# A two-layer encoder trunk on one core: two accumulator banks for the recurrence alone, and its attention and gate work put under it by priority

## The chip, the core and the metric

The kernel runs on one NeuronCore of a Trainium2 chip. The metric is the time of one execution in device microseconds: a median of 1884.04 us in three runs of the kernel before (1882.89 to 1890.43). The engines have short names here: PE is the matrix engine and PEld its weight load, DVE the vector engine, ACT the scalar engine, POOL the GpSimd engine, SP the engine that issues most of the loads.

## The reference

Two layers over 512 tokens of width 1024, all in float32. Cut to what matters:

```python
xn = rms_norm(x, ln1[l]);  z = xn @ w_in[l]
a_q, a_i, a_ff, a_fb, a_g, b_u, b_v, c_q, c_k, c_v, gz = split(z)
# branch A: gated linear recurrence, forward and backward, 4 heads of 128
y_a = rms_norm(hgrn2_bidirectional(a_q, a_i, a_ff, a_fb, lower[l]), a_norm[l]) * silu(a_g)
# branch B: u * (W_s LN(v) + b) with a 128x128 mixing matrix per group
y_b = spatial_gating(gelu(b_u), gelu(b_v), w_s[l], b_s[l])
# branch C: windowed attention, 8 query heads, 2 key heads, blocks of 128, a sink per head
y_c = window_attention(rope(c_q), rope(c_k), c_v, sink[l])
g = sigmoid(gz)                                   # three gates of width 1024
x = x + (g[0]*(y_a @ w_br[l,0]) + g[1]*(y_b @ w_br[l,1]) + g[2]*(y_c @ w_br[l,2])) @ w_out[l]
x = x + square(relu(rms_norm(x, ln2[l]) @ w_up[l])) @ w_down[l]
```

A last rms_norm ends the program.

## The kernel before

**Wide products.** Each float32 operand is split into a rounded high part and the rest, so that a product is three matmuls: high by high, high by rest, rest by high (lines 172 to 174 and 200 to 202). A projection (`proj`, `proj_w`) takes one 128 x 1024 weight chunk and gives one 128 x 512 tile in an accumulator bank tagged "m", by 24 matmuls of 512 columns (12 for a `yB` tile). Its weight chunk is loaded by SP into one of two `wr` buffers, cast by ACT (line 166) and subtracted by DVE (line 168).

**Banks.** The eight accumulator banks are dealt out by tag: "m" for projections (3), "a" for branch A (1), "c" for scores of branch C and parts of the larger products (2), "s" for transposes, norms and the outputs of C (2). A tile takes a bank of its tag and holds it until its last reader is done.

**One layer** runs through four parts: the large token-wise products of the input projection (names tA to gC, pool "G"), the three branches (pool "br"), the merge (pool "Y2": names `y`, `mT`, `wo`), and the MLP (names `up`, `dA` to `dC`). The branch part is where the change lies. It has these pieces:

- **A head of branch A** (`a_ffb`, then `a_head`): two gate projections `f`, one `q`; then eight products `at` of 128 x 128 blocks, one after the other. Between two of them stand an exponential on ACT for `qt` and one for `kt` (lines 513, 516), a multiplication on DVE (514), a masked copy of the product (504) and two in-place updates of `ex` on DVE (541). Then come a transpose `kT`, states `stp`, the output `av`, a norm over ACT, DVE and POOL, and a transpose `oT`. There is one `ex` buffer and one `at` buffer, so the heads follow each other.
- **Branch B**: `gelu2` and a norm of `bv`, mixing products `mx`; its merge, `gz` and `yB` for eight column blocks d, gives `mg`, which POOL stores to memory (`mgd`).
- **Branch C**: four runs j of four blocks n. `c_scores` makes two score tiles `sc` and their softmax (DVE line 831, ACT line 835, DVE 838 to 842); `c_out`, one step later, transposes (`pT`), copies (ACT line 858), multiplies (`po`, line 862) and copies out (864).
- **Gates of A**: four projections `ag` with a tanh.

**What sets the order.** The program is recorded through a scheduler that fills each engine's list by its own time table: of the instructions it holds ready, the one with the lowest priority number is next. The number is the place in the source text; `hp()` lifts a block to the front. The lists are fixed at build time; on the chip every engine takes its list strictly in order, each instruction waiting for its own semaphores. In the source before, the order is head 0, branch B, head 1, branch C whole, head 2, head 3, the merge of B, the gates of A.

## Time and profile before

| what | value |
|---|---|
| median of three runs | 1884.04 us |
| the profiled execution, its own time | 1884.62 us |
| its span, first to last instruction | 1882.8 us |
| PE busy in the span | 1763.8 us, 94% |
| DVE busy | 1316.7 us, 70% |
| ACT busy | 1010.8 us, 54% |
| branch part of layer 0, first `f` to first `y` | 176.4 to 505.5 us |
| branch part of layer 1 | 1077.7 to 1433.8 us |

The span and the profiled execution's own time differ by 1.8 us, which lies around the first and last instruction. Busy time of PE is modelled from overlapping matmuls, so it says where PE waits rather than how much of its rate is used. Views used below: the busy time of each engine in chosen stretches ("windows"), with the granted clock of PE (1.00 is full speed); the list of instructions in order of time ("timeline"), where `x8` counts matmuls, a float32 one as two passes, and the brackets give the idle time ahead of an instruction and what ended it; and groups of like instructions.

### The profile page before, as it was taken

Reading aid. Unit: us, or ns where it says so; the run is one execution under the profiler, and the core shown is the slowest. Engines: PE = TensorE matmul, PEld = TensorE weight load, DVE = VectorE, ACT = ScalarE, POOL = GpSimd, SP = SyncE. Lnnn points to the kernel's source line nnn. Section 1 sums busy time; section 2 is a strip of 40 time slices with the busy share of each in tenths; the row PEclk is TensorE's granted clock in tenths of the full one; section 3 lists DMA queues with packets and bytes.
Section 4 is the critical chain, followed back from the end, with each engine's and each line's share of the span. In section 5 each row is a group of like instructions: output and inputs, shape, how many; then the busy total and the mean of one; then the engine's idle time right before and its main releaser. Section 6 shows DMA issues by size and latency. Waiting matters only on the chain.

```text
span 1882.8 us, 21899 instructions
## 1 busy us (share of the span) xinstructions
PE 1763.8 (94%) x8032; PEld 1435.4 (76%) x8032; DVE 1316.7 (70%) x2006; ACT 1010.8 (54%) x1683; POOL 139.7 (7%) x183
## 2 busy tenths in 40 slices
PE   6999997999699999999989999979978999999997
PEld 4778876887587778888868888758866878888785
DVE  8886885577464767676887679856673656676857
ACT  4555664566323645454565576755772245545453
POOL 3010110000210000000010101101002100000000
PEclk8999997999799999999989999979997999999999
DMA  6242221212253342333334222203214442333221
GB/s 230 90 134 82 86 68 45 90 62 73 85 194 128 108 129 75 123 100 100 128 107 134 81 88 70 76 23 106 84 35 149 153 168 80 122 103 99 96 72 45
DMA packets 54698, 189.34 MB, mean 101 GB/s; under 512 B 7232, under 2 KB 7744, under 8 KB 54592
## 3 DMA queue, kind: packets, MB, share of 16 engines
q1 hardware_dynamic: 43776, 153.35, 24.5%
q0 software_dynamic: 10240, 33.56, 5.1%
q8 instruction: 63, 1.03, 0.2%
q10 hardware_dynamic: 576, 1.05, 0.1%
q14 instruction: 43, 0.35, 0.1%
HBM read 171.15 MB, written 16.78 MB: 100 GB/s over the span
## 4 chain that ended last, share of the span: by engine, by line
PE 61%; issue 25%; DVE 7%; ACT 5%; DMA 1%; POOL 1%; SPq 0%; POOLq 0%; DVEq 0%; ACTq 0%
PE up L174 3%; PE up L172 3%; PE up L173 3%; PE at L499 2%; PE y L200 2%; PE y L201 2%; PE y L202 2%; PE dA L380 2%; PE wo L200 2%; PE dA L381 2%; PE gz L172 2%; PE wo L202 2%; PE wo L201 2%; PE dA L382 2%; PE gz L173 2%
## 5 line engine op out<-in xcount | busy, mean ns | idle before, releaser
L168 DVE TENSOR_TENSOR wl<-wr,wh 128x1024 fp32r<-128x1024 f32 x172 | 210.5, 1224 | 198.7 <-ACT wh L166 198.3
L166 ACT CAST wh<-wr 128x1024 fp32r<-128x1024 f32 x172 | 180.3, 1049 | 289.4 <-PE up L173 101.4
L166 ACT CAST wh<-wq 128x1024 fp32r<-128x1024 f32 x196 | 205.6, 1049 | 228.5 <-PE dA L381 53.7
L168 DVE TENSOR_TENSOR wl<-wq,wh 128x1024 fp32r<-128x1024 f32 x196 | 239.0, 1221 | 119.3 <-ACT wh L166 117.7
L172 PE MATMUL up<-xh,wh 128*128 128x512 f32 x512 | 199.5, 391 | 3.7 <-ACT wh L166 3.7
L173 PE MATMUL up<-xl,wh 128*128 128x512 f32 x512 | 199.9, 390 | 0.0
L174 PE MATMUL up<-xh,wl 128*128 128x512 f32 x512 | 198.8, 390 | 1.1 <-DVE wl L168 1.1
L172 PEld LDWEIGHTS up<-xh,wh 128*128 128x128 f32 x512 | 96.1, 188 | 26.7 <-ACT wh L166 7.1
L174 PEld LDWEIGHTS up<-xh,wl 128*128 128x128 f32 x512 | 96.2, 188 | 21.7 <-DVE wl L168 1.9
L173 PEld LDWEIGHTS up<-xl,wh 128*128 128x128 f32 x512 | 96.2, 188 | 19.9 <-DVE xl L212 0.4
L380 PE MATMUL dA<-wh,sh 128*128 128x512 f32 x256 | 101.9, 398 | 0.2
L381 PE MATMUL dA<-wh,sh 128*128 128x512 f32 x256 | 100.8, 394 | 0.0
L499 PE MATMUL at<-qt,kt 128*128 128x128 f32 x448 | 71.3, 308 | 25.8 <-DVE at L504 8.9
L499 PEld LDWEIGHTS at<-qt,kt 128*128 128x128 f32 x448 | 65.7, 218 | 32.9 <-ACT kt L516 27.9
L382 PE MATMUL dA<-wl,sh 128*128 128x512 f32 x256 | 90.4, 394 | 0.0
L541 DVE TENSOR_TENSOR ex<-ex 128x512 f32<-128x512 f32 x112 | 76.8, 703 | 7.2 <-ACT kt L516 6.5
L229 POOL TENSOR_TENSOR rs<-ms,mhalf_t 128x4 f32<-128x4 f32 x13 | 16.6, 1273 | 638.7 <-DVE ms L227 616.0
L380 PEld LDWEIGHTS dA<-wh,sh 128*128 128x128 f32 x256 | 48.1, 188 | 14.6 <-ACT wh L166 3.7
L513 ACT ACTIVATE qt<-ex 128x512 f32<-128x512 f32 x56 | 37.8, 675 | 38.9 <-DVE ex L541 34.6
L831 DVE CUSTOM_DVE_ANT_0 sc<-sc,cmask_t,snk_t 128x256 f32<-128x256 f32 (+1 forms) x64 | 34.5, 545 | 33.9 <-PE pT L857 33.7
L382 PEld LDWEIGHTS dA<-wl,sh 128*128 128x128 f32 x256 | 48.1, 188 | 10.9
L381 PEld LDWEIGHTS dA<-wh,sh 128*128 128x128 f32 x256 | 48.3, 189 | 10.6
(383 smaller groups left out, 4471.2 us busy)
## 6 DMA issues: line engine op xcount, KB each, us to landing
wr<-in_ws_dram SPq DMA_DIRECT2D x172, 512.0 KB, 3.3
wq<-in_ws_dram SPq DMA_DIRECT2D x112, 512.0 KB, 4.3
thd<-zt POOLq DMA_DIRECT2D x32, 256.0 KB, 2.7
th<-thd POOLq DMA_DIRECT2D x32, 256.0 KB, 4.4
mgd<-mg POOLq DMA_DIRECT2D x16, 256.0 KB, 2.4
mB<-mgd POOLq DMA_DIRECT2D x16, 256.0 KB, 3.5
x<-in_xT_dram SPq DMA_DIRECT2D x8, 256.0 KB, 7.3
xr<-in_xt_dram POOLq DMA_DIRECT2D x8, 256.0 KB, 5.2
```

Source lines behind the costliest of these rows:

```text
L166: nc.scalar.copy(hi, raw)
L168: nc.vector.tensor_tensor(lo, raw, hi.bitcast(F32), ALU.subtract)
L172: nc.tensor.matmul(pt, whi, xhi, start=first, stop=False)
L173: nc.tensor.matmul(pt, whi, xlo, start=False, stop=False)
L174: nc.tensor.matmul(pt, wlo, xhi, start=False, stop=last)
L200: nc.tensor.matmul(pts[t], xh, hi[:, c], start=k == 0, stop=False)
L201: nc.tensor.matmul(pts[t], xl, hi[:, c], start=False, stop=False)
L380: nc.tensor.matmul(pts[p], xh[:, t], hi[:, c], start=start and k == 0, stop=False, skip_group_check=True)
L381: nc.tensor.matmul(pts[p], xl[:, t], hi[:, c], start=False, stop=False, skip_group_check=True)
L382: nc.tensor.matmul(pts[p], xh[:, t], lo[:, c], start=False, stop=k == 3, skip_group_check=True)
L499: nc.tensor.matmul(pt[:, c], kk(st), qq[:, c], start=True, stop=True)
L541: nc.vector.tensor_tensor(o_ap, o_ap, ap_of(ex, i_, [[istep, 2]] + z), ALU.add)
```

## The change

The change rewrites the order of the branch part and deals the banks anew.

- Banks: "m" goes from 3 to 2, "a" from 1 to 2. The large products take two "a" banks where they took one "m" and one "a".
- `a_head` gets a second `at` buffer.
- A class `later(n)` raises the priority number of what stands in it, so that it is placed behind text that follows it. Runs of branch C stand in `later(15000)`, the eight parts of B's merge (`merge_b`) and the gates of A (`gate_a`) in `later(30000)`.
- In the source the order is now: head 0, branch B and its split, head 1, C's keys and values, merge part 0, run 0, head 2, parts 1 and 2, run 1, part 3, head 3, part 4, run 2, parts 5 to 7, run 3, the last `c_out`, the gates of A.
- The gates' tiles move from tag "tv" to "l2". In the merge branch A is taken first and C second, where it was C and then A; the splits swap their pools (A's into Y2's "yi", C's into Y1's "yh").

The number of instructions is the same on every engine (7526 on PE, 1998 on DVE, 1561 on ACT with the table loads, 188 on POOL, 306 on SP), and so is each kind.

```diff
--- before.py
+++ after.py
@@ -82,8 +82,8 @@
 
     HOME = {t: p for p, ts in {"G": ("xs", "zt"), "Y1": ("yh",), "br": ("q", "a", "g", "ch"), "Y2": ("yi", "th", "mg"), "mlp": ("h",)}.items() for t in ts}
     part = {}
-    BANKS = {"m": 3, "a": 1, "c": 2, "s": 2}
-    GROUPS = (("m", "m", "c", "c"), ("m", "a", "s", "s"))
+    BANKS = {"m": 2, "a": 2, "c": 2, "s": 2}
+    GROUPS = (("m", "m", "c", "c"), ("a", "a", "s", "s"))
     WR, WB, NZ, NCT, NSM, NQ = 2, 2, 3, 4, 4, 10
 
     def nm(s):
@@ -114,6 +114,19 @@
         return ps.tile([P, S], F32, tag="p_" + tag, bufs=BANKS[tag], name=nm(name))
 
     hp = tc.high_priority
+
+    class later:
+
+
+        def __init__(self, n):
+            self.n = n
+
+        def __enter__(self):
+            tc.cur_priority += self.n
+
+        def __exit__(self, *e):
+            tc.cur_priority -= self.n
+
     cnt = [0]
 
 
@@ -397,7 +410,7 @@
                 V.tensor_tensor(b11[i], t1[i], b22[i], ALU.add)
         product(6, b11, pa, False)
         read("P16", pa)
-        pc = [PT("m", name + "C"), PT("a", name + "C")]
+        pc = [PT("a", name + "C") for _ in range(2)]
         product(7, t3, pc, True)
         read("P7", pc)
         product(5, t1, pa, False)
@@ -490,7 +503,7 @@
         return ex
 
     def a_head(l, h, ex, q, vt):
-        at = part["br"].tile([P, 4, P], F32, tag="at", bufs=1, name=nm("at"))
+        at = part["br"].tile([P, 4, P], F32, tag="at", bufs=2, name=nm("at"))
 
         def attn(kk, qq):
             pt = PT("a", "at")
@@ -768,9 +781,41 @@
             nc.vector.scalar_tensor_tensor(bu[g], y, 0.5, bu[g], ALU.mult, ALU.mult)
             yb.append(bu[g])
 
+        def y_split(ys, tag):
+            res = []
+            for y in ys:
+                hi, lo = T(tag, "yh", F32R), T(tag, "yl", F32R)
+                split(y, hi, lo)
+                res.append((hi, lo))
+            return res
+
+
+        ys = y_split(yb, "yh")
+        wbr = [None]
+
+        def merge_b(d):
+            z = evac(proj(xs, "gz", l, "gz", d), "z", "gz")
+            with hp():
+                nc.scalar.activation(z, z, AF.Tanh, scale=0.5)
+            if d % 2 == 0:
+                wbr[0] = wload(l, "yb", d // 2)
+            yp = proj_w(ys, "yB", wbr[0], (d % 2) * 4)
+            m = T("g", "mg")
+            with hp():
+                nc.vector.scalar_tensor_tensor(m, z, 1.0, yp, ALU.add, ALU.mult)
+            nc.gpsimd.dma_start(mgd[:, d], m)
+
+        sg = []
+
+        def gate_a():
+            z = evac(proj(xs, "ag", l, "ag", len(sg)), "l2", "ag")
+            th = T("jk", "th")
+            nc.scalar.activation(th, z, AF.Tanh, scale=0.5)
+            nc.vector.scalar_tensor_tensor(z, th, 1.0, z, ALU.add, ALU.mult)
+            sg.append(z)
+
         g1 = a_ffb(1)
         q1 = evac(proj(xs, "q", l, "q", 1), "q", "q")
-
         oa.append(a_head(l, 1, g1, q1, vt))
 
 
@@ -863,52 +908,42 @@
             for h, r in enumerate((lo64, hi64)):
                 nc.scalar.copy(yc[j][r, n * P:(n + 1) * P], po[r, h * P:(h + 1) * P])
 
+        def fill(*ds):
+            with later(30000):
+                for d in ds:
+                    merge_b(d)
+
+        def c_run(j):
+            nonlocal prev
+            with later(15000):
+                qs = c_q(j)
+                for n in range(4):
+                    cur = c_scores(j, n, qs)
+                    if prev is not None:
+                        c_out(*prev)
+                    prev = cur
+
         prev = None
-        for j in range(4):
-            qs = c_q(j)
-            for n in range(4):
-                cur = c_scores(j, n, qs)
-                if prev is not None:
-                    c_out(*prev)
-                prev = cur
-        c_out(*prev)
-
+        fill(0)
+        c_run(0)
         g2 = a_ffb(2)
         q2 = evac(proj(xs, "q", l, "q", 2), "q", "q")
         oa.append(a_head(l, 2, g2, q2, vt))
-
+        fill(1, 2)
+        c_run(1)
+        fill(3)
         g3 = a_ffb(3)
         q3 = evac(proj(xs, "q", l, "q", 3), "q", "q")
         oa.append(a_head(l, 3, g3, q3, vt))
-
-        def y_split(ys, tag):
-            res = []
-            for y in ys:
-                hi, lo = T(tag, "yh", F32R), T(tag, "yl", F32R)
-                split(y, hi, lo)
-                res.append((hi, lo))
-            return res
-
-
-        ys = y_split(yb, "yh")
-        for d in range(KT):
-            z = evac(proj(xs, "gz", l, "gz", d), "z", "gz")
-            with hp():
-                nc.scalar.activation(z, z, AF.Tanh, scale=0.5)
-            if d % 2 == 0:
-                wbr = wload(l, "yb", d // 2)
-            yp = proj_w(ys, "yB", wbr, (d % 2) * 4)
-            m = T("g", "mg")
-            with hp():
-                nc.vector.scalar_tensor_tensor(m, z, 1.0, yp, ALU.add, ALU.mult)
-            nc.gpsimd.dma_start(mgd[:, d], m)
-        sg = []
-        for h in range(4):
-            z = evac(proj(xs, "ag", l, "ag", h), "tv", "ag")
-            th = T("jk", "th")
-            nc.scalar.activation(th, z, AF.Tanh, scale=0.5)
-            nc.vector.scalar_tensor_tensor(z, th, 1.0, z, ALU.add, ALU.mult)
-            sg.append(z)
+        fill(4)
+        c_run(2)
+        fill(5, 6, 7)
+        c_run(3)
+        with later(15000):
+            c_out(*prev)
+        with later(30000):
+            for h in range(4):
+                gate_a()
         end("br")
         begin("Y2")
 
@@ -923,7 +958,7 @@
                 th = []
                 for t in range(4):
                     z = T("th", "th")
-                    nc.gpsimd.dma_start(z, thd[:, bi * 4 + t, fl * S:(fl + 1) * S])
+                    nc.gpsimd.dma_start(z, thd[:, (1 - bi) * 4 + t, fl * S:(fl + 1) * S])
                     th.append(z)
                 pts = proj_tok(ys, f"y{br}", (l, "y", br, fl), grp)
                 grp ^= 1
@@ -948,10 +983,10 @@
                             split(m, hi, lo)
                         ms[d] = (hi, lo)
 
-        gated(0, 2, y_split(yc, "yi"))
         for h in range(4):
             nc.vector.scalar_tensor_tensor(oa[h], oa[h], 0.5, sg[h], ALU.mult, ALU.mult)
-        gated(1, 0, y_split(oa, "yh"))
+        gated(0, 0, y_split(oa, "yi"))
+        gated(1, 2, y_split(yc, "yh"))
 
 
         xr = [[T("l", "xr"), T("l", "xr")] for _ in range(4)]
```

How the lists move, at three places of PE's list in the branch part of layer 0. The names: `at` is a level of a head of branch A, `kT`, `stp`, `av`, `oT` are its end; `q`, `gz`, `yB` are projections, `pT`, `sc`, `po` belong to branch C, `y` to the merge. "x4" are four matmuls that follow each other.

Head 1, before. The eight levels stand one behind the other, and the head's end behind them:

```order
L499 MATMUL at_1803<-qt_1798,kt_1801 128x128 x4
L499 MATMUL at_1813<-q_1795,dg_1811 128x128 x4
L499 MATMUL at_1826<-qt_1821,kt_1824 128x128 x4
L499 MATMUL at_1839<-qt_1834,kt_1837 128x128 x4
L499 MATMUL at_1852<-qt_1847,kt_1850 128x128 x4
L499 MATMUL at_1865<-qt_1860,kt_1863 128x128 x4
L499 MATMUL at_1878<-qt_1873,kt_1876 128x128 x4
L499 MATMUL at_1894<-qt_1889,kt_1892 128x128 x4
L556 MATMUL kT_1908<-id_t,kd_1906 128x128 x3
L561 MATMUL stp_1914<-vt_453,kT_1912 128x128
L561 MATMUL stp_1914<-vt_455,kT_1912 128x128
L561 MATMUL stp_1914<-vt_527,kT_1912 128x128
```

Head 1 in the change, around its third and fourth level:

```order
L187 MATMUL q_2430<-xh_156,wl_2428 128x512
L185 MATMUL q_2430<-xh_164,wh_2426 128x512
L512 MATMUL at_1842<-qt_1837,kt_1840 128x128 x4
L186 MATMUL q_2430<-xl_165,wh_2426 128x512
L187 MATMUL q_2430<-xh_164,wl_2428 128x512
L902 MATMUL pT_2300<-id_t,sc_2246 128x128 x3
L512 MATMUL at_1855<-qt_1850,kt_1853 128x128 x4
L185 MATMUL gz_2640<-xh_110,wh_2636 128x512
L186 MATMUL gz_2640<-xl_111,wh_2636 128x512
L185 MATMUL yB_2668<-yh_1690,wh_2182 128x512
L186 MATMUL yB_2668<-yl_1691,wh_2182 128x512
L187 MATMUL yB_2668<-yh_1690,wl_2184 128x512
```

Projections stand between the levels now. From the second to the last level there are 20, 2, 36, 24, 14 and 22 wide matmuls of `q`, `gz`, `yB` and `cq` between neighbours, and a few of C's; the gap of two wide ones is the one shown.

The end of the branch part, before. Behind the last pieces of head 3 stands its transpose, and then the merge at once:

```order
L584 MATMUL av_3382<-st_3356,qd_3360 128x128
L584 MATMUL av_3382<-st_3375,qd_3379 128x128
L584 MATMUL av_3382<-vt_529,at_3235 128x128
L584 MATMUL av_3382<-st_3356,qd_3360 128x128
L596 MATMUL oT_3405<-id_t,ao_3403 128x128 x4
L200 MATMUL y_884_4024<-wh_4030,yh_4000 128x512
L200 MATMUL y_885_4025<-wh_4030,yh_4000 128x512
```

In the change C follows the same transpose of head 3:

```order
L609 MATMUL oT_3262<-id_t,ao_3260 128x128 x4
L902 MATMUL pT_3504<-id_t,sc_3448 128x128 x3
L902 MATMUL pT_3509<-id_t,sc_3453 128x128 x3
L873 MATMUL sc_3726<-k_447_2127,q_796_3681 128x384
L874 MATMUL sc_3726<-kl_2129,q_796_3681 128x384
L907 MATMUL po_3514<-pT_3503,cvt_2144 128x256 x3
L902 MATMUL pT_3710<-id_t,sc_3487 128x128 x2
```

and the merge starts behind C's last block:

```order
L907 MATMUL po_3793<-pT_3782,cvt_2144 128x256 x3
L902 MATMUL pT_3822<-id_t,sc_3766 128x128 x3
L902 MATMUL pT_3827<-id_t,sc_3771 128x128 x3
L907 MATMUL po_3832<-pT_3821,cvt_2144 128x256 x3
L902 MATMUL pT_3839<-id_t,sc_3805 128x128 x2
L902 MATMUL pT_3843<-id_t,sc_3810 128x128 x2
L907 MATMUL po_3847<-pT_3838,cvt_2144 128x256 x2
L213 MATMUL y_884_4028<-wh_4034,yh_4004 128x512
L213 MATMUL y_885_4029<-wh_4034,yh_4004 128x512
```

Six outputs of C (`po`) with their transposes, and six of the score tiles, now stand between head 3's `oT` and the first `y`. In layer 1 it is six outputs too. Before, C's last three outputs stood between the first levels of head 3.

## The prediction

> **What bounds the kernel now.** I read the page first, then the windows of the branch part, then its timeline.
>
> ```profile
> span 1882.8 us, 21899 instructions
> PE   6999997999699999999989999979978999999997
> PEclk8999997999799999999989999979997999999999
> PE 61%; issue 25%; DVE 7%; ACT 5%; DMA 1%; POOL 1%; SPq 0%; POOLq 0%; DVEq 0%; ACTq 0%
> ```
>
> PE and its own issue make 86% of the chain, so time is won only where PE stands still or runs slowly. Outside the first slice the busy row dips in few places, and PEclk dips with it: both lie in the branch parts. Windows of those (layer 0: rows 1 to 4, layer 1: 5 to 8) and one of the MLP:
>
> ```profile
> core 0: us, PE busy (x) PEld busy (x) DVE busy (x) ACT busy (x) POOL busy (x), PEclk, DMA share, GB/s
> 177.00:300.00 123.00, 119.90 (x596) 100.85 (x595) 95.04 (x160) 73.68 (x121) 17.33 (x12) 0.99 0.27 90
> 300.40:329.45 29.05, 17.07 (x74) 14.38 (x72) 18.87 (x30) 13.51 (x27) 0.00 (x0) 0.57 0.06 18
> 329.45:463.00 133.55, 132.37 (x675) 111.79 (x676) 84.84 (x195) 83.78 (x199) 9.11 (x12) 0.98 0.22 75
> 463.00:505.50 42.50, 25.52 (x139) 20.65 (x137) 24.49 (x49) 22.01 (x60) 1.73 (x3) 0.81 0.04 13
> 1077.00:1227.90 150.90, 146.13 (x722) 122.02 (x721) 121.44 (x210) 100.94 (x157) 18.14 (x16) 0.99 0.25 81
> 1227.90:1256.20 28.30, 17.07 (x73) 14.15 (x72) 18.73 (x31) 14.85 (x28) 0.00 (x0) 0.65 0.10 34
> 1256.20:1394.40 138.20, 133.52 (x694) 112.45 (x692) 89.63 (x203) 95.88 (x216) 10.07 (x12) 0.98 0.22 73
> 1394.40:1435.70 41.30, 25.48 (x121) 20.76 (x122) 22.48 (x45) 20.03 (x56) 3.71 (x6) 0.74 0.07 23
> 860.00:880.00 20.00, 20.00 (x90) 16.55 (x89) 10.11 (x15) 9.26 (x15) 0.00 (x0) 1.00 0.37 127
> ```
>
> The last row gives the price of a wide matmul that nothing holds up: about 88 starts in 20 us, 0.227 us. Each layer has a **bare stretch** (rows 2 and 6: 29.05 and 28.30 us), where head 1 runs alone, and a **tail** (rows 4 and 8: 42.5 and 41.3 us), where head 3 runs with the last of C. The rest is full. Inside the bare stretch of layer 0, in order of time:
>
> ```profile
> 302.23 1.13 PE L499 MATMUL at<-q,dg 128*128 128x128 f32 x8 [0.77 <-ACT at L519]
> 304.81 2.05 PE L499 MATMUL at<-qt,kt 128*128 128x128 f32 x8 [1.45 <-DVE at L504]
> 308.35 2.05 PE L499 MATMUL at<-qt,kt 128*128 128x128 f32 x8 [1.49 <-DVE qt L514]
> 311.76 2.05 PE L499 MATMUL at<-qt,kt 128*128 128x128 f32 x8 [1.36 <-DVE at L504]
> 328.71 0.68 DVE L627 TENSOR_TENSOR q<-q,rb 128x512 f32<-128x512 f32 x1
> 329.45 0.79 PE L172 MATMUL gz<-xh,wh 128*128 128x512 f32 x1 [1.17 <-DVE q L627]
> 334.74 0.63 PE L172 MATMUL gz<-xh,wh 128*128 128x512 f32 x1
> 335.76 0.39 PE L172 MATMUL gz<-xh,wh 128*128 128x512 f32 x1
> ```
>
> Every level waits on DVE or ACT (the brackets), 3.4 us from one to the next (308.35 to 311.76), while its eight matmuls need about 0.9 us at full clock. Projections could have run there: the next, `gz`, waited for a bank (329.45, released by DVE line 627, the read of head 3's `q` at 328.71). All three "m" banks were held by projections whose readers waited for head 1 to free its buffers. After the stretch the wide matmuls run 0.43 us apart until about 335.2.
>
> **The change part by part.** No work is added or removed, so each stretch is worth its length less the work in it.
>
> *The bare stretches go.* In the lists, 2 to 36 wide matmuls now stand between head 1's levels. Layer 0: 29.05 us hold eight levels (7.2 us), three `kT` and six `stp` matmuls (0.85): 21.0 us are lost now. From 329.4 to 335.2, 14 matmuls take 5.8 us where 14 x 0.227 = 3.2 would do: 2.6 more. Layer 1: the 73 matmuls of row 6 are six levels (5.4 us), the same nine (0.85) and 16 wide ones (3.6): 18.4 of 28.3 us lost, and some ten slow matmuls behind it, 2.0. Together **-44.0 us**. The fill is no new work: it comes out of 329 to 463, which is full (PE busy 132.4 of 133.6 us), and shortens that by its own length. That a level with cover costs nothing, head 0 shows:
>
> ```profile
> 208.44 1.06 PE L499 MATMUL at<-q,dg 128*128 128x128 f32 x8
> 214.58 1.06 PE L499 MATMUL at<-qt,kt 128*128 128x128 f32 x8
> ```
>
> 6.1 us apart, no idle bracket.
>
> *The tails are dealt anew.* Head 3's end now, and C's steps where little else runs:
>
> ```profile
> 481.06 1.13 PE L499 MATMUL at<-qt,kt 128*128 128x128 f32 x8 [1.48 <-DVE qt L514]
> 484.57 1.16 PE L499 MATMUL at<-qt,kt 128*128 128x128 f32 x8 [2.38 <-ACT kt L516]
> 486.89 0.90 PE L556 MATMUL kT<-id_t,kd 128*128 128x128 f32 x3 [1.16 <-ACT at L533]
> 491.15 0.90 PE L556 MATMUL kT<-id_t,kd 128*128 128x128 f32 x3 [1.15 <-DVE st L568]
> 495.42 0.80 PE L584 MATMUL av<-vt,at 128*128 128x128 f32 x2 [1.15 <-DVE st L568]
> 503.16 1.09 PE L596 MATMUL oT<-id_t,ao 128*128 128x128 f32 x4 [3.40 <-DVE ao L592]
> 505.53 2.08 PE L200 MATMUL y<-wh,yh 128*128 128x512 f32 x4 [1.28 <-ACT yh L208]
> ```
>
> ```profile
> 1380.51 1.13 PE L862 MATMUL po<-pT,cvt 128*128 128x256 f32 x4
> 1383.39 1.03 PE L862 MATMUL po<-pT,cvt 128*128 128x256 f32 x4
> 1394.46 1.56 PE L862 MATMUL po<-pT,cvt 128*128 128x256 f32 x6 [1.23 <-ACT pT L858]
> 1398.50 1.56 PE L862 MATMUL po<-pT,cvt 128*128 128x256 f32 x6 [0.93 <-ACT pT L858]
> ```
>
> In the change the fill ends (last `ag`) with two levels of head 3 left in layer 0, one in layer 1. Layer 0: first level 0.4, next 3.5, to `kT` 2.3, to `av` 8.5, to `oT` 7.7, its own 1.1. The second "a" bank saves some 1.5, since the second `kT` no longer waits for the states' reads (491.15). That is 22.0 us. Then six outputs of C stand in PE's list before the merge. A two-block step takes 2.9 us (1380.51 to 1383.39), a three-block one 4.0, both at full clock; three of each make 20.7. At half clock their matmuls on the chain (about 1.0 and 1.6 us) double: 28.5. I take 24, between them, since PEclk is 0.81 and 0.74 in today's tails. With 1.3 for the first cast before `y` (505.53), 47.3 us. It holds 20.9 us of work: two levels 1.8, the head's end 4.2, 20 `po` products 8.6 (1.03 us covered a row of four passes), 40 transposes 3.3, ten score tiles 3.0. Lost: 26.4. Today's 42.5 us hold 16.9 (eight levels, three steps, the same end): 25.6. So +0.8. Layer 1: 43.7 less 20 is 23.7, against 41.3 less 13.8, 27.5: -3.8. Together **-3.0 us**; the bounds of a step's price make it -10 to +6.
>
> *New tight places.* A level needs 2.4 us between the end of the one before and its start (1.5 after the `dg` product, 304.81; `kT` 1.4 after the last level). Where the list has less cover, PE waits for the rest. Layer 0: 0.7 us of cover at the fourth level of head 1 (two wide matmuls, three transposes): 1.7; 0.4 at head 2's third: 1.1; `kT` of heads 0, 1 and 2 with 0, 0 and 1.1: 3.1. Layer 1 has five such places, 4.5. Together **+10.4 us**. Below lies 0, if cover elsewhere is longer than the chain needs; above 25, if the stretch loses as 177 to 300 does (its DVE is 77% busy) and these places besides.
>
> *One "m" bank fewer.* A read of a projection takes 0.68 us (328.71), and between a projection's end and the next but one's start stand 4 to 9 us of matmuls in most cases, 1.3 at least (`yB`). In the MLP the third `up` product must now wait for the first one's reader:
>
> ```profile
> 616.76 1.08 ACT L1018 ACTIVATE u<-up 128x512 f32<-128x512 f32 x2
> 616.91 0.50 PE L172 MATMUL up<-xh,wh 128*128 128x512 f32 x1 [0.43 <-ACT wh L166]
> ```
>
> That reader starts at 616.76, half of the pair; the third product starts at 616.91. So 0.5 us a layer, **+1.0**. If readers get late the cost is the rival below.
>
> *At nothing:* the swap of A and C in the merge (the same 192 matmuls a layer; both casts still precede the first `y`), the gates' tiles in "l2" (`bu` is split by then), the same number of table loads on ACT. SP brings weight chunks in another order, but one per 5.5 us of PE work as now. POOL's store of `mg` waits for DVE, and a head's `rs` and `dg` are queued behind it; head chains have cover except in the tail, where no store is left. If a store were late there, a head would slip by its 1 to 3 us.
>
> Sum: -44.0 - 3.0 + 10.4 + 1.0 = -35.6 us. Against the profiled execution's own 1884.62 us (median of the runs 1884.04, the same within 0.6) that is **1849 us**.
>
> **The clock, by the page.** In the bare stretch PE's idle gaps were 1.4 to 1.5 us (the brackets from 304.81 on), and still the granted clock fell to half:
>
> ```profile
> 305.00:310.00 5.00, 3.52 (x16) 3.25 (x16) 2.83 (x5) 1.64 (x3) 0.00 (x0) 0.50 0.09 35
> 310.00:320.00 10.00, 6.09 (x25) 5.29 (x25) 7.60 (x12) 3.88 (x7) 0.00 (x0) 0.50 0.00 0
> ```
>
> The Trainium skill ("TensorE: Matmul & The Clock Gate", section "Part 1: The HAM clock gate (the "warmup" mystery)") has the clock halved after at least one idle window of about 3.4 us. By that rule no gap of the new tail would halve it. The rows speak against so strict a reading.
>
> **Rivals.**
> - *The tail stays at full clock.* For it: today's tail holds 1.00 while C's steps are between the levels. Against: head 3's end runs at half there. Steps at 20.7 instead of 24 save 6.6 us in two layers, the head's end at full clock 4.2 a layer: **1834**. It is also what the page's rule would give.
> - *DVE becomes the bound under head 3*, whose levels now share it with C's steps, the weights and the gates.
>
> ```profile
> L541 DVE TENSOR_TENSOR ex<-ex 128x512 f32<-128x512 f32 x112 | 76.8, 703 | 7.2 <-ACT kt L516 6.5
> ```
>
> Between its first and seventh level DVE's list in the change holds 34 instructions of this size (23 of the head, 11 of the gates; 0.70 each), four subtractions twice as wide (1.4) and some 6 us of small ones of C: 35 us, where PE's list holds 27. For it: the neighbouring levels have 4 to 5 us of cover, no more. Against: 0.70 is latency, and neighbours overlap. If the head slips by the 8 us in each layer, **1865**.
> - *Two banks block (the slower side).* Two projections with late readers now suffice to hold PE, where it took three (329.45). Each such block costs what the bare stretch did, 21.0 + 2.6 us. One a layer gives back the gain and more: 1849 + 47 = **1896**; it decides from one block in each layer. Against: DVE's list has the reads of head 2's and 3's gate projections at the start of the head before, not behind its levels.
> - *The fill is in the list but late* (weights, casts): the bare stretch comes back elsewhere, **1884**.
>
> **How the numbers follow.** Forecast 0.62, full clock 0.10, DVE 0.15, blocks 0.07, no effect 0.06. A measurement of this kernel can tell about 0.5% (9.4 us) from no change. Faster 0.62 + 0.10 + 0.15 = 0.87, same 0.06, slower 0.07. The range takes in the tail's bounds (-7 to +9), the tight places' (-10 to +15) and the two faster rivals: 1828 to 1870.
>
> **What would show it.** Right: no stretch of head 1 with PE under 70% busy, PEclk near 1.00 from the first `f` to the last `ag`; one tail a layer of 44 to 47 us, in which six `po` rows follow head 3's `oT` 3 to 5 us apart; idle before `at` and `kT` of some 10 us in the covered part. Wrong: idle before a projection released by DVE line 640 or 648 (a bank), DVE over 90% busy under head 3, or a tail far from 45 us.

## The result, and the profile after

The changed kernel takes 1836.15 us in the median of four runs (1833.48 to 1836.94), the kernel before 1885.6 us beside it. The ratio is 0.9733, with a 95% interval of 0.9709 to 0.9756: faster by 2.7%, some 49 us. The profiled execution took 1836.94 us, 47.7 less than the one before; the prediction had 35.6 less. From the changed kernel's page (span, two rows of the slices, the chain by engine):

```profile
span 1835.2 us, 21898 instructions
PE   5999999998799999999989999999979999999997
PEclk7999999999899999999989999999999999999999
PE 59%; issue 21%; DVE 10%; ACT 7%; DMA 2%; POOL 0%; SPq 0%; POOLq 0%; DVEq 0%; ACTq 0%
```

Each layer had two dips of the busy row and now has one. The windows of the branch part of the changed kernel, cut at head 1 and at the last `ag` (rows 1 to 4 layer 0, 5 to 8 layer 1; columns as in the prediction):

```profile
182.70:300.00 117.30, 115.76 (x599) 98.20 (x598) 90.16 (x158) 75.47 (x126) 11.52 (x10) 1.00 0.26 88
300.00:345.00 45.00, 45.00 (x238) 38.39 (x237) 29.35 (x46) 25.21 (x48) 5.61 (x6) 1.00 0.29 99
345.00:438.60 93.60, 91.13 (x500) 78.63 (x498) 78.39 (x158) 61.36 (x137) 7.86 (x8) 1.00 0.22 74
438.60:487.70 49.10, 33.73 (x155) 25.72 (x153) 22.23 (x74) 29.85 (x96) 2.87 (x5) 0.79 0.09 28
1057.40:1200.00 142.60, 138.41 (x695) 116.71 (x694) 115.44 (x202) 99.08 (x157) 13.70 (x14) 0.98 0.24 81
1200.00:1253.50 53.50, 51.66 (x270) 43.20 (x269) 38.08 (x56) 35.45 (x61) 5.49 (x6) 1.00 0.26 90
1253.50:1346.50 93.00, 92.50 (x504) 79.38 (x501) 79.10 (x162) 65.71 (x148) 8.63 (x8) 1.00 0.21 74
1346.50:1387.40 40.90, 27.42 (x136) 20.40 (x134) 18.71 (x64) 26.73 (x85) 2.90 (x5) 0.92 0.10 33
```

From the first `f` to the last `ag` the clock is full and PE is busy for 251.9 of 255.9 us in layer 0: the bare stretch is gone. What is left is the tail (49.1 and 40.9 us). Inside it, head 3's end and C's steps in layer 0 (timeline of PE):

```profile
462.42 1.12 PE L609 MATMUL oT<-id_t,ao 128*128 128x128 f32 x4 [3.27 <-DVE ao L605]
467.03 2.76 PE L907 MATMUL po<-pT,cvt 128*128 128x256 f32 x6
471.68 1.13 PE L907 MATMUL po<-pT,cvt 128*128 128x256 f32 x4
...
482.73 1.56 PE L907 MATMUL po<-pT,cvt 128*128 128x256 f32 x6 [0.87 <-ACT pT L903]
485.81 1.13 PE L907 MATMUL po<-pT,cvt 128*128 128x256 f32 x4 [0.46 <-ACT pT L903]
487.69 0.50 PE L213 MATMUL y<-wh,yh 128*128 128x512 f32 x1 [0.75 <-ACT yh L221]
```

Six steps stand between `oT` and the first `y`, 3.1 to 4.7 us apart, 23.4 us in all (from the end of `oT` to the end of the last `po`). The time by pieces of the two profiled executions (boundaries: first `f`, last `ag`, first `y`, first `up` of each layer):

| piece | before | forecast | after |
|---|---|---|---|
| start to first `f`, layer 0 | 176.4 | 176.4 | 182.7 |
| first `f` to last `ag`, layer 0 | 286.6 | 264.9 | 255.9 |
| tail, layer 0 | 42.5 | 47.3 | 49.1 |
| first `f` to last `ag`, layer 1 | 316.7 | 294.6 | 289.1 |
| tail, layer 1 (to the first `y`) | 39.4 | 43.7 | 40.9 |
| first `y` to first `up`, both layers | 195.7 | 193.8 | 192.2 |
| the rest, MLP and layer 1's input products | 825.5 | 826.5 | 825.3 |

The forecast of the covered pieces is the old length less the bare stretch's loss, plus the tight places, less the work that moves into the tail: 286.6 - 23.6 + 5.9 - 4.0, and 316.7 - 20.4 + 4.5 - 6.2. The 193.8 is there because the prediction's row of layer 1's tail ran to 1435.7, 1.9 us into the merge. Layer 1 of the kernel before is cut where the prediction cut it, at 1394.4; its last `ag` ended at 1390.15 already, so that by the name of the row 4.3 us of its 316.7 belong to the tail (43.6 instead of 39.4).

### The profile page after: what moved, and what is told of

Same layout as the page of the kernel before. It is cut to its first block, busy times and chain, and to the rows that moved or that the text cites. A ratio compares the mean times of both kernels' runs of the same rounds, so it can differ in the third digit from the quotient of the medians.

```text
span 1835.2 us, 21898 instructions
## 1 busy us (share of the span) xinstructions
PE 1743.1 (95%) x8032; PEld 1420.4 (77%) x8032; DVE 1315.4 (72%) x2006; ACT 1009.2 (55%) x1683; POOL 135.4 (7%) x183
## 4 chain that ended last, share of the span: by engine, by line
PE 59%; issue 21%; DVE 10%; ACT 7%; DMA 2%; POOL 0%; SPq 0%; POOLq 0%; DVEq 0%; ACTq 0%
PE up L185 3%; PE up L187 3%; PE up L186 3%; DVE wl L181 2%; PE dA L393 2%; PE y L213 2%; PE at L512 2%; PE y L215 2%; PE y L214 2%; PE dA L394 2%; PE dA L395 2%; PE gA L395 2%; PE gA L393 1%; PE gA L394 1%; PE wo L213 1%
## 5 line engine op out<-in xcount | busy, mean ns | idle before, releaser
L512 PEld LDWEIGHTS at<-qt,kt 128*128 128x128 f32 x448 | 58.3, 194 | 8.2 <-ACT kt L529 3.2
L512 PE MATMUL at<-qt,kt 128*128 128x128 f32 x448 | 60.6, 279 | 3.6 <-ACT kt L529 2.1
L185 PE MATMUL gz<-xh,wh 128*128 128x512 f32 x128 | 51.3, 400 | 3.0 <-ACT wh L179 3.0
```

Of the source, the lines that this page charges most:

```text
L185: nc.tensor.matmul(pt, whi, xhi, start=first, stop=False)
L512: nc.tensor.matmul(pt[:, c], kk(st), qq[:, c], start=True, stop=True)
```

## The experiments

The change has two halves, the banks and the order. Neither the result nor the profile after tells which of them won, so each was run alone.

**The banks alone.** On the kernel before:

```diff
-    BANKS = {"m": 3, "a": 1, "c": 2, "s": 2}
-    GROUPS = (("m", "m", "c", "c"), ("m", "a", "s", "s"))
+    BANKS = {"m": 2, "a": 2, "c": 2, "s": 2}
+    GROUPS = (("m", "m", "c", "c"), ("a", "a", "s", "s"))
-        pc = [PT("m", name + "C"), PT("a", name + "C")]
+        pc = [PT("a", name + "C") for _ in range(2)]
-        at = part["br"].tile([P, 4, P], F32, tag="at", bufs=1, name=nm("at"))
+        at = part["br"].tile([P, 4, P], F32, tag="at", bufs=2, name=nm("at"))
```

> The kernel before with the banks of the change alone (two "m", two "a", the second group, the seventh product's pair, two `at` tiles); the order of the source, the priorities and the gates' tiles stay as before. Theory O (the order fills the bare stretches, as the prediction has it): head 1 still runs alone, the levels still wait on DVE and ACT, 3.4 us apart; the two bare stretches of 29.05 and 28.30 us stay, and the start is 6.3 us longer, as in the changed kernel (first `f` at 182.7 instead of 176.4): 1885 + 6 = 1891 us. Theory B (the second "a" bank lets the heads go on without waiting for the reader of the product before, and with it the list deals the projections differently): by its list four levels of head 1 stay bare in layer 0 (4 x 2.5 us idle), few in layer 1, but C is through before head 3 ends and the gates' projections stand beside head 3's end, so that the tails of 42.5 and 41.3 us shrink to some 15 us: 1836 or below, 1815 to 1845 us.

1828.3 us (1825.3 to 1830.1), ratio to before 0.9688 (0.9675 to 0.9701): faster than the whole change. Windows of its layer 0, cut at head 1's bare part and the last `ag`:

```profile
182.60:299.00 116.40, 114.04 (x578) 96.14 (x577) 95.39 (x163) 75.38 (x125) 16.59 (x12) 0.99 0.26 86
299.00:324.50 25.50, 16.33 (x79) 13.76 (x78) 16.86 (x30) 11.53 (x26) 0.00 (x0) 0.72 0.13 42
324.50:468.80 144.30, 144.30 (x778) 123.83 (x778) 102.24 (x231) 99.64 (x238) 9.08 (x12) 0.99 0.22 74
468.80:481.60 12.80, 7.99 (x57) 6.87 (x55) 5.76 (x12) 6.33 (x21) 1.84 (x3) 0.98 0.13 42
```

The bare stretch is still there (25.5 us against 29.05); the tail of 42.5 us has become 12.8, at a clock of 0.98. C ends before head 3 does, and the gates' projections stand beside head 3's last products.

**The order alone.** On the changed kernel, the three lines of banks and of the pair `pc` put back:

```diff
-    BANKS = {"m": 2, "a": 2, "c": 2, "s": 2}
-    GROUPS = (("m", "m", "c", "c"), ("a", "a", "s", "s"))
+    BANKS = {"m": 3, "a": 1, "c": 2, "s": 2}
+    GROUPS = (("m", "m", "c", "c"), ("m", "a", "s", "s"))
...
-        pc = [PT("a", name + "C") for _ in range(2)]
+        pc = [PT("m", name + "C"), PT("a", name + "C")]
```

> The changed kernel with the banks of before (three "m", one "a"); the lower priorities, the source order, the gates in "l2" and the merge's order stay changed. Theory O: the bare stretches are gone all the same; the start is 6.3 us shorter again (third `bu` has its bank) and the `up` products 1 us: 1836 - 7 = 1829 us, with some idle before `at` and `kT`. Theory B: with one bank the waits before `kT` and after the `dg` product are back (1.1 to 1.5 us each, ten or more of them a layer), and the list leaves six levels of head 3 after the last projection; each costs 2.5 us more than under cover, 15 us a layer: about 1829 + 30 = 1859 us, with a stretch of 60 us and more after the last `ag` of each layer.

1896.4 us (1894.8 to 1898.2), ratio 1.0051 (1.0037 to 1.0065): half a percent slower than before, and 37 us beyond even theory B's 1859. No bare stretch is left in front (before the rows shown, PE is busy for 239 of 244 us), but all of that and more stands behind the last `ag`, in layers 0 and 1:

```profile
421.10:510.00 88.90, 57.57 (x277) 45.30 (x274) 46.86 (x129) 49.43 (x147) 5.54 (x7) 0.77 0.05 15
1352.60:1445.20 92.60, 59.46 (x277) 47.56 (x275) 48.04 (x131) 55.89 (x153) 5.72 (x7) 0.76 0.05 15
```

So the four corners are 1885.6 (neither), 1828.3 (banks), 1896.4 (order) and 1836.2 (both). With either order the banks are worth 57 to 60 us; with either banks the new order costs 8 to 11.

**Which bank.** The banks differ in two ways, one "m" fewer and one "a" more. On the kernel of banks_alone, the heads were held to one of the two "a" banks:

```diff
-    BANKS = {"m": 2, "a": 2, "c": 2, "s": 2}
-    GROUPS = (("m", "m", "c", "c"), ("a", "a", "s", "s"))
+    BANKS = {"m": 2, "a": 1, "x": 1, "c": 2, "s": 2}
+    GROUPS = (("m", "m", "c", "c"), ("a", "x", "s", "s"))
-        pc = [PT("a", name + "C") for _ in range(2)]
+        pc = [PT("a", name + "C"), PT("x", name + "C")]
```

> The kernel of banks_alone, but the heads' products and transposes may use only one of the two "a" banks; the other takes part in the token groups and the seventh product alone, so that everything outside the branch part keeps its banks, and "m" keeps its two. Theory B (the second bank of the heads is what wins: with one, a head's next product waits for the reader of the last, and the list is dealt for the longer heads): bare stretches and tails of the kernel before come back, and the 6.3 us at the start stay: 1886 + 6 = 1892 us, rather more, since only two projections can be ahead. Theory M (two "m" banks instead of three win, because projections of the next heads no longer run ahead of those that could serve as cover): 1828 us stay.

1896.8 us (1895.6 to 1897.1), ratio 1.0060 (1.0043 to 1.0076). The second bank of the heads is the whole gain. The second `at` tile is in this kernel and in order_alone too, so it wins nothing by itself; the bank without that tile was not run. Layer 0's waits of PE in this kernel (line waited for, us in total, times, longest):

```profile
PE at L499 <- DVE at L504: 6.6, 6, 1.4
...
PE q L172 <- DVE z L635: 4.6, 2, 2.8
...
PE kT L556 <- ACT at L533: 1.7, 2, 0.8
...
PE kT L556 <- DVE st L568: 1.1, 1, 1.1
```

The first, third and fourth are waits for the reader of the product before, in the one bank; the second is the "two banks block" of the prediction's rivals, which shows here and, but for 0.3 us in layer 1, not in the changed kernel. In banks_alone none of the first, third and fourth is left in layer 0.

**What the new order costs, and by which part.** On the changed kernel (banks, gates in "l2" and A first in the merge kept), the source order and the priorities were undone; then the new places kept without lower priorities; then the lower priorities kept on the old places.

```diff
-            with later(30000):
+            with later(0):
...
-            with later(15000):
+            with later(0):
...
         prev = None
-        fill(0)
         c_run(0)
+        c_run(1)
+        c_run(2)
+        c_run(3)
+        with later(0):
+            c_out(*prev)
         g2 = a_ffb(2)
...
         oa.append(a_head(l, 3, g3, q3, vt))
...
+        fill(0,1,2,3,4,5,6,7)
+        with later(0):
             for h in range(4):
                 gate_a()
```

This is the edit of order_undone, in which the calls that stood between and behind heads 2 and 3 are gone from there. Places_alone has its `later(0)` with the calls left where the change has them; priorities_alone has its places with 15000 and 30000.

> The changed kernel with its banks, gates in "l2" and A first in the merge, but with the order of the source and the priorities of before (all of C, heads 2 and 3, B's merge, the gates, none at lower priority). It differs from banks_alone only in the gates' tiles and the merge. If the order and the priorities are what the changed kernel pays over banks_alone (1836.2 against 1828.3 us): 1828 us, with the bare stretch of head 1 in layer 0 (about 25 us) and tails of some 13 us. If the gates' tiles and the merge's order cost it: 1836 us. If they win something by themselves, because A's `y` needs no wait for C: 1825 us.

> The changed kernel with no lower priorities: C's runs and B's parts keep their new places in the source, between the heads, at the priority of their place. If the places cost the 12 us that the changed kernel needs over order_undone (C's third and fourth run stand behind head 3 in the source, and their list still has six steps of C behind head 3's `oT`): 1836 us, with tails of some 45 us. If the lower priorities cost them: 1824 us, with C through before head 3 ends.

> order_undone with the lower priorities of the change (C by 15000, B's merge and the gates by 30000) on the source order of before, in which all of C stands ahead of heads 2 and 3. If the places cost the 12 us: near 1824 us; in its list two steps of C, not six, stand behind head 3's `oT`, 3.5 us each in a tail (the row spacing of C's steps behind head 3 in the changed kernel), so 1824 + 2 x 3 = about 1830 us at most. If the lower priorities cost them: 1836 us.

| kernel | us | ratio to before |
|---|---|---|
| the change | 1836.2 | 0.9733 (0.9709 to 0.9756) |
| places_alone | 1833.3 | 0.9721 (0.9706 to 0.9736) |
| order_undone | 1824.2 | 0.9678 (0.9663 to 0.9693) |
| priorities_alone | 1820.3 | 0.9653 (0.9638 to 0.9667) |

Where the places are new the time is 1833 to 1836 us, where they are old 1820 to 1824, so the cost is in the places: C's third and fourth run stand behind head 3 in the source, and with or without the lower priority six steps of C are left behind head 3's `oT` (none in order_undone, two and one in priorities_alone). The lower priorities by themselves cost nothing; whether they win the 4 us the intervals leave open. Order_undone against banks_alone (0.9688) differs in the gates' tiles, the merge's order and the place of branch B's split, which stands ahead of head 1: the intervals overlap, so the three together are worth nothing measurable; for the first two the prediction had said so.

**The start.**

```diff
-            return [evac(proj(xs, "bu", l, "bu", i), "l2", "bu") for i in range(4)]
+            return [evac(proj(xs, "bu", l, "bu", i, bank="a" if l == 0 and i > 1 else "m"), "l2", "bu") for i in range(4)]
```

Not shown is the argument `bank`, which `proj` and `proj_w` get and hand on to the tile.

> The changed kernel, but in layer 0 the third and fourth `bu` projection, at the program's start, take an "a" bank, which nothing else uses yet. If the 6.3 us that the changed kernel loses before its first `f` (182.7 against 176.4) come from the third `bu` waiting for an "m" bank (idle of 2.65 us before `bc` and 1.40 us before `bu`, released by DVE line 640, and the slow matmuls behind), they come back: first `tA` at some 53 us, first `f` at some 176.5, 1836 - 6 = 1830 us. If the later start is that of the loads or of the run, nothing changes: 1836 us.

1829.0 us, ratio 0.9693 (0.9679 to 0.9706), 7.2 below the change. The start in the timeline of the kernel before:

```profile
39.09 0.77 PE L172 MATMUL bu<-xh,wh 128*128 128x512 f32 x1
45.96 1.05 PE L236 MATMUL bc<-id_t,rs 128*128 128x128 f32 x8
47.08 0.50 PE L380 MATMUL tA<-wh,xh 128*128 128x512 f32 x1
```

In that of the changed kernel:

```profile
42.11 2.07 PE L249 MATMUL bc<-id_t,rs 128*128 128x128 f32 x8 [2.65 <-POOL rs L242]
45.59 0.80 PE L185 MATMUL bu<-xh,wh 128*128 128x512 f32 x1 [1.40 <-DVE bu L640]
59.21 0.39 PE L393 MATMUL tA<-wh,xh 128*128 128x512 f32 x1
```

And in that of start_bank:

```profile
46.70 1.05 PE L249 MATMUL bc<-id_t,rs 128*128 128x128 f32 x8
53.06 0.39 PE L393 MATMUL tA<-wh,xh 128*128 128x512 f32 x1
```

Before, the third `bu` filled the time in which the norm's small chain (`cs` to `bc`) runs; with two "m" banks it stands behind `bc`, waits for a reader and runs its first twelve matmuls at half clock, where before it was six. With an "a" bank it is back in front.

**Cover for the tail.** A's half of the merge could run in the tail if its split did not wait for memory of the branch part:

```diff
-        gated(0, 0, y_split(oa, "yi"))
-        gated(1, 2, y_split(yc, "yh"))
+        gated(0, 0, y_split(oa, "yh"))
+        gated(1, 2, y_split(yc, "yi"))
-    GROUPS = (("m", "m", "c", "c"), ("a", "a", "s", "s"))
+    GROUPS = (("m", "m", "a", "a"), ("c", "c", "s", "s"))
...
-                        pt = PT("s" if grp == 0 else "c", "mT")
+                        pt = PT("s" if grp == 0 else "a", "mT")
```

> The changed kernel, but A's half of the merge splits its input into the "yh" tiles, which branch B's merge has left long before, instead of "yi", whose memory is free only when the branch part ends; C takes "yi"; the first group of banks is m, m, a, a, the second c, c, s, s, and the `mT` transposes take "a" after the first. In its list 54 to 66 of A's `y` matmuls stand between head 3's `oT` and C's last `po`. Theory 1 (the tail behind head 3 is C's chain of waits, with PE some 11 of 23 us unused and the clock at half until 470.9 in layer 0): `y` fills the waits, and 8 to 10 us a layer are won: 1836 - 18 = 1818 us. Theory 2 (PE takes its list in order, and each group of twelve `y`, 2.7 us, holds C's next step up longer than the 0.3 to 1.2 us that it waits now): only the idle in front of each step is won, 3 us a layer: 1830 us; 1836 or more would say that C's chain is lengthened by as much as is moved.

1831.5 us, ratio 0.9709 (0.9696 to 0.9722): 4.7 below the change, near theory 2's 1830; the two intervals overlap, so that by the times alone the gain is not certain. From the first `f` to the first `up` it wins 5.4 us in layer 0 and 2.4 in layer 1, where some 15 us of `y` work stand in each of C's tails.

**Cover for head 1.** In order_undone, B's merge spread over the source:

```diff
         c_run(0)
         c_run(1)
+        fill(0)
         c_run(2)
         c_run(3)
         with later(0):
             c_out(*prev)
+        fill(1,2)
         g2 = a_ffb(2)
...
+        fill(3,4)
         g3 = a_ffb(3)
...
-        fill(0,1,2,3,4,5,6,7)
+        fill(5,6,7)
```

> As order_undone, but B's merge, at ordinary priority, is dealt over the source: part 0 behind C's second run, 1 and 2 behind C, 3 and 4 behind head 2, 5 to 7 behind head 3. Theory L (with two "a" banks what is left in banks_alone is head 1's bare stretch, 25.5 us in layer 0 with 16.3 us of PE busy, and some 14 us in layer 1, whose levels find no cover only because B's merge comes later in the source): two thirds of the loss there are won, 9 + 6 us, and the fill taken away makes the tails some 3 us longer each: 1828 - 9 = 1819 us. Theory Z (cover moved forward is missing behind, one for one): 1828 us.

1826.7 us, ratio 0.9691 (0.9674 to 0.9708), no better than order_undone: theory Z. Head 1's stretch and the tail of layer 0 in the windows of order_undone:

```profile
299.00:325.00 26.00, 17.17 (x77) 14.27 (x76) 17.94 (x33) 12.75 (x26) 0.00 (x0) 0.69 0.11 39
...
467.20:479.30 12.10, 8.11 (x58) 6.74 (x56) 6.13 (x13) 6.89 (x22) 1.82 (x3) 1.00 0.14 45
```

The same two in b_spread:

```profile
299.00:325.00 26.00, 22.79 (x115) 18.29 (x115) 14.60 (x21) 15.05 (x24) 0.54 (x1) 1.00 0.21 71
...
450.20:480.20 30.00, 18.47 (x115) 15.38 (x113) 16.95 (x41) 20.66 (x61) 1.82 (x3) 0.93 0.06 18
```

The idle time of the first row (8.8 us, at a clock of 0.69) fell to 3.2; that of the tail rose from 4.0 to 11.5. The cover was moved, not made.

**New cover behind it.** C is through before head 3 ends in these kernels, so it is C's `y` that can stand beside head 3's end. Merge_and_banks gives order_undone that merge (C first, its halves in "yh", A's in "yi") and the start's "a" banks; spread_and_banks adds the spread; all_with_priorities adds the lower priorities as well, and moves part 0 of B's merge from behind C's second run to behind C.

```diff
-                    nc.gpsimd.dma_start(z, thd[:, (1 - bi) * 4 + t, fl * S:(fl + 1) * S])
+                    nc.gpsimd.dma_start(z, thd[:, bi * 4 + t, fl * S:(fl + 1) * S])
...
-        gated(0, 0, y_split(oa, "yi"))
-        gated(1, 2, y_split(yc, "yh"))
+        gated(0, 2, y_split(yc, "yh"))
+        gated(1, 0, y_split(oa, "yi"))
```

> spread_and_banks without the spread: order_undone with the "a" banks for the third and fourth `bu` and with C first in the merge, in the "yh" tiles. If the spread is worth nothing by itself (b_spread 1826.7 against order_undone 1824.2) and nothing here either: 1801 us as well. If the spread pays as soon as C's `y` products stand behind as cover in its place: the bare stretch of head 1 is back (some 12 us lost in layer 0, 8 in layer 1), and the time is 1801 + 15 = 1816 us.

> As b_spread, with the "a" banks for the third and fourth `bu` projection of layer 0 (start_bank), and C first in the merge, its halves in the "yh" tiles, A's in "yi": C is through before head 3 ends, so that its `y` products can stand beside head 3's end; in the list 24 to 60 of them come before the last `oT`. Theory L: the start gives 6 us and the `y` cover the 10 us or so that each tail loses, at full clock: b_spread less 6 and less 12, about 1800 us. If `y` again only takes the idle and lengthens the chain beside it, as in a_merge_early (1831.5 against 1836.2): b_spread less 10, about 1809 us. Without any effect of the merge: b_spread less 6.

> spread_and_banks (1801.4 us) with the change's lower priorities (C by 15000, B's parts and the gates by 30000) and part 0 behind C instead of behind C's second run. If the priorities win the 4 us that priorities_alone showed against order_undone (1820.3 against 1824.2) here too: 1797 us. If the spread and the `y` products have taken that already, or C's later steps take the cover of head 3's end away: 1801 us or some microseconds more.

1815.8 us (0.9627, 0.9608 to 0.9645), **1801.4 us** (0.9554, 0.9540 to 0.9569) and 1812.8 us (0.9601, 0.9580 to 0.9621). Spread_and_banks beats the change by 35 us. The spread, worth nothing in b_spread, is worth 14 here by the medians. Between the profiled executions 8.8 and 2.7 us of the difference lie between the first `f` and the first `up` of the two layers, where C's `y` now stands in the place from which the spread took cover away; 2.5 lie at the start, where the lists are alike, and are not the spread's. The tail of spread_and_banks, from the last `ag` to the end of head 3's `oT`:

```profile
443.50:477.70 34.20, 31.58 (x178) 27.04 (x177) 19.08 (x42) 21.68 (x61) 1.02 (x1) 0.95 0.09 31
```

PE is busy for 31.6 of 34.2 us there, part of them `y`, against 33.7 of 49.1 in the change. All_with_priorities is 11 us longer; 2.8 of them lie at the start, where the lists are alike. In layer 0 C's last `po` stands behind head 3's `oT` and ends 307 us after the first `f` instead of 293, so that its `y` can end only later; which part of the rest is the priorities' and which the place of part 0 was not run apart.

## Why the prediction was right, and where not

**The bare stretches go, -44.0: right for the whole change, and put down to the wrong half.** The prediction saw in the lists that the fill stands between head 1's levels, which is so (PE busy 45.00 of 45.00 us). It took the order for the cause and gave the second "a" bank 1.5 us. The order alone moves the same cover to the front and takes it from the back: 1896.4 us, where the prediction's account gives some 1829 (theory O). The second bank wins 57 to 60 us. The size came out because the prediction read the finished lists, in which the bank's effect is already contained; that the number is near says nothing for the account of which half wins.

**The step that failed** is "New tight places", +10.4. It priced the wait after the `dg` product (1.5) and the one before `kT` (1.4) from rows of the kernel before, as latency of the head. Those rows were waits for the reader of the one "a" bank (for the second `kT` the prediction saw this, and gave the bank its 1.5 us), and the releaser in their brackets says so: DVE line 504 and ACT line 533 read the product out. Layer 0's waits of PE before, in the whole branch part, among others:

```profile
PE at L499 <- DVE at L504: 5.4, 4, 1.5
...
PE kT L556 <- ACT at L533: 2.0, 2, 1.2
...
PE at L499 <- ACT at L519: 1.2, 2, 0.8
PE gz L172 <- DVE q L627: 1.2, 1, 1.2
PE kT L556 <- DVE st L568: 1.1, 1, 1.1
```

After, from the first `f` to the last `ag` of layer 0, these are all the waits of PE:

```profile
PE gz L185 <- ACT wh L179: 2.5, 1, 2.5
PE at L512 <- ACT kt L529: 1.3, 1, 1.3
PE f L185 <- ACT wh L179: 0.2, 1, 0.2
```

In the timeline there, `kT` follows head 0's last level with no idle time:

```profile
247.72 1.06 PE L512 MATMUL at<-qt,kt 128*128 128x128 f32 x8
248.61 0.49 PE L569 MATMUL kT<-id_t,kd 128*128 128x128 f32 x3
...
285.69 1.16 PE L512 MATMUL at<-qt,kt 128*128 128x128 f32 x8 [1.33 <-ACT kt L529]
```

The one tight place of head 1 that was really latency, its fourth level, was forecast at 1.7 and came at 1.33. In place of 10.4 us of such waits before `at` and `kT` there were 1.3 in layer 0 and 1.2 in layer 1, some 8 us fewer. The covered pieces came out 9.0 and 5.5 us under the forecast (the table above), 14.5 together, and the windows say where the rest went: in the four covered rows of the kernel before PE stood idle for 13.7 us, which the forecast left as they were and raised by 10.4; in the six covered rows after it stands idle for 10.5 us in all, 13.6 less. That is more than the 12 us by which the forecast was too slow; the start took 6.3 of it back.

**The tails** were right: 90.0 us together where 91.0 was forecast, C's six steps 23.4 and 22.3 us where 24 was taken. Layer 0 was slower before `oT` (8.8 us from `av` to `oT` instead of 7.7), layer 1 faster (6.9).

**One "m" bank fewer, +1.0**, was mis-sized. In the MLP of layer 0 the third `up` is held, for 0.95 us where 0.5 was forecast, and the pieces outside the branch parts and merges are no longer for it (825.3 against 825.5). But at the program's start, which the prediction did not look at, the third `bu` costs 6.3 us.

**Not foreseen** was the merge, 3.5 us shorter in two layers. The prediction put it at nothing; the 1.9 us in the table come from where its row ended, and are luck. The first four `y` matmuls behind C's last steps take 1.19 us in layer 0 (487.69), where behind head 3's end they took 2.08 (505.53), at half clock. Steps of C ahead do not always do that: in layer 1 of order_alone and places_alone the first four take 2.08 and 2.04.

**The rivals.** DVE under head 3 was busy 78.4 of 93.6 us, 84%, not the 90% that it would have taken. Blocked banks came to 0.3 us in layer 1. The tail at full clock was neither right nor wrong: 0.79 and 0.92 on average, and the prediction's reading that no gap there would halve the clock did not hold (below). That the time came near this rival's 1834 is chance; what brought it there was the idle time that did not come.

**What stays open.** The waits for the one bank that the trace names make some 10 us in layer 0 before (the four rows above without `gz`: 9.7) and 7.2 in layer 1, 17 of the 57 to 60 us. The rest came through the lists: with one bank the scheduler deals C and the projections so that nothing is left for the last head. That is read from the lists and the tails of 88.9 and 12.8 us; no run had one kernel's list with the other's banks, so the two shares are not measured apart.

## What to carry to other kernels

Give a serial chain two accumulator banks before reordering the work around it: a bracket that names the reader of the product before is a wait for a bank, not latency. One bank or two was 1896.8 against 1828.3 us here. The Trainium skill ("Perfetto Trace Analysis", section "Matmuls") has independent matmul groups rotate through banks, so that the reading of one overlaps the matmuls of the next; these runs agree, with the 68.5 us between those two times, for the products of one chain. Cover that is moved to one bare stretch was missing in another here until new work was found to stand behind. When a change has two halves, run each alone: this one's halves were worth -57 and +11 us, and the best version kept the first and, of the order, a spread of B's merge alone.

## What the runs showed of the hardware

The clock fell to half without any long idle time of PE. In the tail of layer 1 of the changed kernel (windows of PE, the third column from the end being the granted clock):

```profile
1346.50:1348.50 2.00, 1.69 (x13) 1.25 (x11) 1.60 (x3) 1.98 (x6) 0.00 (x0) 1.00 0.02 4
1348.50:1350.50 2.00, 0.60 (x4) 0.36 (x4) 2.00 (x7) 1.96 (x7) 0.00 (x0) 1.00 0.00 0
1350.50:1352.50 2.00, 1.78 (x6) 1.40 (x7) 1.61 (x6) 1.97 (x6) 0.00 (x0) 0.79 0.70 215
1352.50:1354.50 2.00, 2.00 (x8) 1.73 (x8) 0.53 (x1) 1.52 (x6) 0.00 (x0) 0.50 0.15 55
```

And the timeline there:

```profile
1346.91 1.16 PE L512 MATMUL at<-qt,kt 128*128 128x128 f32 x8 [0.21 <-ACT kt L529]
1347.91 0.49 PE L902 MATMUL pT<-id_t,sc 128*128 128x128 f32 x3
1348.98 0.55 PE L569 MATMUL kT<-id_t,kd 128*128 128x128 f32 x3 [0.58 <-ACT kd L566]
1350.45 0.39 PE L873 MATMUL sc<-k,q 128*128 128x256 f32 x1 [0.92 <-DVE mx L876]
```

The longest gap is 0.92 us, and PE's busy share over 1348.5 to 1350.5 is 30%; the 0.79 of the next row puts the halving about 1.2 us later. From the end of the last `at` product (1348.07) to 1350.45 only six transposes ran; whether transposes count as work for the clock no run here tells. The Trainium skill ("TensorE: Matmul & The Clock Gate", section "Part 1: The HAM clock gate (the "warmup" mystery)") has the clock halved after an idle window of about 3.4 us; the rows differ from it, with 0.92 us of idle, or 2.4 if the transposes are left out.

Two executions with the same list of PE at the start (spread_and_banks and merge_and_banks) reached their first `f` at 176.3 and 178.8 us, so a single profile's start is known to some 2.5 us.
